# A routed-expert layer on one core: the query projection split into two passes, with gathers in the second

## The chip, the cores and the metric

The kernel runs on one core of a Trainium2 chip. The metric is device time in microseconds (us); lower is better. The core has the engines PE (matrix products), DVE and ACT (elementwise work), POOL (elementwise work, and the issue of gathers) and SP (which here issues most DMAs). Each engine works through its instructions in a fixed order.

## What is computed

One decoder layer on 512 tokens of width 2048 in float32: attention with two groups of heads, then PEER, a layer of 16384 experts of one neuron each. The edit lies in PEER. Per token, 8 heads each pick 16 experts by product keys:

```python
q = (xt @ w_query).reshape(T, PEER_HEADS, 2, PEER_HALF)        # 2048 -> 16 x 128
scores = jnp.einsum('thpc,hpnc->thpn', q, sub_keys)            # 128 keys for each half
vals, idx = lax.top_k(scores, PEER_TOPK)
cand = vals[..., 0, :, None] + vals[..., 1, None, :]
top_vals, top_c = lax.top_k(cand.reshape(T, PEER_HEADS, 256), PEER_TOPK)
experts = i1 * PEER_N_KEYS + i2                                # 128 experts a token
gates = jax.nn.softmax(top_vals, axis=-1)
...
hdn = jax.nn.gelu(jnp.einsum('ted,td->te', expert_down[ec], xc))
y = jnp.einsum('te,ted->td', gc * hdn, expert_up[ec])
```

## The kernel before, in words

The 512 tokens are four blocks of 128. Matrix products are made with three passes of a split operand: `load_split` loads a raw piece of 128x1024 weights, ACT writes its rounded part `hi` (L93), and DVE or POOL writes the remainder `lo` (L94); `mm3` then runs lo by hi, hi by lo and hi by hi (L99 to L101). One ring of buffers, the pool `wts` (three raw, two hi, two lo), serves all weights up to the expert-up weights.

PEER works in two ways at once. The first 320 tokens meet all 16384 experts as dense products: 128 down tiles of 128 experts (`down_tile`, PSUM tile `dn`, 48 matmuls of 320 columns), then up products (`up`) against the activations times a dense gate matrix. The last 192 tokens gather their own experts' rows: the last 64 tokens of block 2 (list "e", spread over 128 partitions, 64 steps for each table) and block 3 (list "g", 128 steps for each table). One `gather_step` issues an indirect DMA of 128 rows, 1 MiB, from POOL (L511), and one DVE instruction of 2048 columns uses them (L517 for down rows, L525 for up rows). There are 384 steps. Four row buffers rotate; a step is tied in order to a matmul that is passed to it.

The stages that matter, as they are written:

- Choosing. For each of 8 heads, `queries(hp)` projects all 512 tokens for one half-key (48 matmuls of 512 columns into `pq`), keeps the columns of blocks 0 and 1 in `kept` and hands those of blocks 2 and 3 on as `qt`. `choose` makes scores (L562), takes the top 16 on DVE (MAX8, MATCH_REPLACE8, FIND_INDEX8; L539 to L543), forms candidates (L577), takes their top 16 and looks their numbers up (L587 to L590; half of the L589 products are on POOL). Blocks 2 and 3 of head hh are chosen, then blocks 0 and 1 of head hh - 1. The lists for the gathers are whole after the last head of blocks 2 and 3 (L618 to L623).
- Gates. For 10 chunks of 32 tokens, DVE makes one-hot tiles (L680, L681), ACT scales them, PE multiplies them (`gm`) and ACT copies them to a staging tile that goes to DRAM. One gather step in each of the 40 rounds.
- 28 down tiles whose results are spilled to DRAM (both `lo` pieces on POOL), then 10 that are held (`lo` on POOL and DVE, one gather step each).
- The expert loop, 16 groups of 16 slots: each slot loads 512 KiB of up weights and makes 24 matmuls of 320 columns; in every second of the first 180 slots a down tile is made as well, in the other 76 slots a spilled one is loaded back. Gather steps are issued at 1.6 a slot, then 0.8. The last quarter of the last group closes the output rows.

The written order is not the order of the engines: the framework in which the kernel is written lays out each engine's instructions ahead of the run, and places a later instruction earlier where its inputs and buffers allow it.

Of the kernel before, what the change touches and what calls it, by code (L numbers as in the profile page):

```python
# [8 lines left out]
F32 = mybir.dt.float32  # L9
# [9 lines left out]
P = 128  # L19
S = 512  # L20
NB = S // P
D = 2048
NK = D // P
# [6 lines left out]
PH = 8  # L30
TK = 16
HK = PH * TK
NE1 = 128
NEXP = NE1 * NE1
GC = 32
# [4 lines left out]
GB = NB - 1  # L40
NE = 64
EB = GB - 1
RB = 2
E0 = P - NE
ER = P // NE
EH = 128 // ER
HOLD = 10
SPILL = 28
# [11 lines left out]
def peer_block(ctx, tc, x, x_t, w_qk, w_v, w_fg, w_o, w_pq, sub_keys, down_t, down, up_t, up,  # L60
# [17 lines left out]
    ahead = []  # L78

    def fetch(src, pool):  # L80
        raw = pool.tile([P, 1024], F32, tag="raw", name="raw", bufs=3)
        DMA.dma_start(raw, src)
        return raw

# [354 lines left out]
    def aux(name):  # L439
        return psum.tile([P, S], F32, tag="aux", name=name, bufs=4)  # L440
# [89 lines left out]
    with tc.tile_pool(name="route", bufs=1, side="right") as rp:  # L530
        iota = rp.tile([P, NCAND], F32, name="iota_c")
        G.iota(iota, pattern=[[1, NCAND]], base=0, channel_multiplier=0, allow_small_or_imprecise_dtypes=True)
        sk = rp.tile([P, 2 * PH, NE1], F32, name="sk")
        DMA.dma_start(sk, sub_keys)

        def top16(vals, idx, src, width, nm):

            rest = rp.tile([P, width], F32, tag=f"rest{width}", name=f"rest_{nm}", bufs=3)
            V.max(vals[:, 0:8], src)  # L539
            V.match_replace(rest, vals[:, 0:8], src, NEG)  # L540
            V.max(vals[:, 8:16], rest)
            V.max_index(idx[:, 0:8], vals[:, 0:8], src)
            V.max_index(idx[:, 8:16], vals[:, 8:16], rest)  # L543

        def gate_exp(hh, bs):

            t = top[:, bs, hh]
            tmx = rp.tile([P, RB, 1], F32, name="tmx", bufs=2)
            V.tensor_copy(tmx, t[:, :, 0:1])
            V.tensor_tensor(t, t, tmx.broadcast_to([P, RB, TK]), ALU.subtract)  # L550
            A.activation(t, t, AF.Exp)

        def choose(hh, b0, queries):

            bs = slice(b0, b0 + RB)
            vals, idxf = [], []
            for half in range(2):
                hp = 2 * hh + half
                qt = queries(hp)
                sc = aux(f"sc{hp}{b0}")  # L560
                for b in range(RB):
                    PE.matmul(sc[:, b * P:(b + 1) * P], qt[:, b * P:(b + 1) * P], sk[:, hp], start=True, stop=True)  # L562
                vv = rp.tile([P, RB, TK], F32, name="vv", bufs=4)
                ii = rp.tile([P, RB, TK], U32, name="ii", bufs=2)
                for b in range(RB):
                    top16(vv[:, b], ii[:, b], sc[:, b * P:(b + 1) * P], P, f"{hp}{b0}{b}")
                fi = rp.tile([P, RB, TK], F32, name="fi", bufs=4)
                V.tensor_scalar(fi, ii, 128.0 if half == 0 else 1.0, None, ALU.mult)
                vals.append(vv)
                idxf.append(fi)  # L570
            cand = rp.tile([P, RB, NCAND], F32, name="cand", bufs=2)
            cex = rp.tile([P, RB, NCAND], F32, name="cex", bufs=2)
            for dst, (a, b) in ((cand, vals), (cex, idxf)):
                o = 0
                for i, n, m in CAND:
                    dd = dst[:, :, o:o + n * m].rearrange("p b (n m) -> p b n m", n=n)
                    V.tensor_tensor(dd, a[:, :, i:i + n].unsqueeze(3).broadcast_to([P, RB, n, m]),  # L577
                                    b[:, :, 0:m].unsqueeze(2).broadcast_to([P, RB, n, m]), ALU.add)
                    o += n * m
            pos = rp.tile([P, RB, TK], U32, name="pos", bufs=2)  # L580
            for b in range(RB):
                top16(top[:, b0 + b, hh], pos[:, b], cand[:, b], NCAND, f"c{hh}{b0}{b}")
            posf = rp.tile([P, RB, TK], F32, name="posf", bufs=2)
            V.tensor_copy(posf, pos)
            for b in range(RB):
                oh = rp.tile([P, TK, NCAND], F32, name="oh", bufs=2)
                V.tensor_tensor(oh, iota.unsqueeze(1).broadcast_to([P, TK, NCAND]),  # L587
                                posf[:, b].unsqueeze(2).broadcast_to([P, TK, NCAND]), ALU.is_equal)
                (V if hh == PH - 1 or b % 2 else G).tensor_tensor(oh, oh, cex[:, b].unsqueeze(1).broadcast_to([P, TK, NCAND]), ALU.mult)  # L589
                V.tensor_reduce(ex[:, b0 + b, hh], oh, AX.X, ALU.add)  # L590
            if hh:
                gate_exp(hh - 1, bs)
            if hh == PH - 1:
                gate_exp(hh, bs)
                den = rp.tile([P, RB, PH], F32, name="den", bufs=2)
                V.tensor_reduce(den, top[:, bs], AX.X, ALU.add)
                V.reciprocal(den, den)
                V.tensor_tensor(top[:, bs], top[:, bs], den.unsqueeze(3).broadcast_to([P, RB, PH, TK]), ALU.mult)

        kept = rp.tile([P, 2 * PH, RB * P], F32, name="kept")  # L600

        def queries(hp):
            ps = aux(f"pq{hp}")
            for piece in range(2):
                hi, lo = load_split(w_pq[hp, :, piece * 1024:(piece + 1) * 1024], G if hp else V)
                for kk in range(8):
                    k = piece * 8 + kk
                    sl = slice(kk * P, (kk + 1) * P)
                    mm3(ps, (hi[:, sl], lo[:, sl]), (hn[0][:, :, k], hn[1][:, :, k]), k == 0, k == NK - 1)
            qt = rp.tile([P, RB * P], F32, name="qt", bufs=2)  # L610
            A.copy(qt, ps[:, RB * P:])
            A.copy(kept[:, hp], ps[:, :RB * P])
            return qt


        for hh in range(PH):
            choose(hh, NB - RB, queries)
            if hh == PH - 1:  # L618
                for dst, src in ((gidx_e, ex), (gate_e, top)):
                    for r in range(ER):  # L620
                        V.tensor_copy(dst[r * NE:(r + 1) * NE], src[E0:, EB].rearrange("p h k -> p (h k)")[:, r * EH:(r + 1) * EH])
                V.tensor_copy(gidx, ex[:, GB])
                V.tensor_copy(gate_g, top[:, GB].rearrange("p h k -> p (h k)"))  # L623
            if hh:
                choose(hh - 1, 0, lambda hp: kept[:, hp])
        choose(PH - 1, 0, lambda hp: kept[:, hp])
    if "ex" in dbg:
        DMA.dma_start(dbg["ex"], ex)
        DMA.dma_start(dbg["gate"], top)
# [69 lines left out]
    with tc.tile_pool(name="exp", bufs=1, side="right") as xp:  # L699
# [78 lines left out]
        due = 0.0  # L778
# [16 lines left out]
        for g in range(NE1 // NG):  # L795
# [8 lines left out]
            for c in range(NK):  # L804
                raw = xp.tile([P, NG, P], F32, tag="uraw", name="uraw", bufs=3)
                DMA.dma_start(raw, up_t[g, c])
                uh = xp.tile([P, NG, P], F32R, tag="uhi", name="uhi", bufs=2)
                ul = xp.tile([P, NG, P], F32R, tag="ulo", name="ulo", bufs=2)
                A.activation(uh, raw, AF.Copy)  # L809
                V.tensor_tensor(ul, raw, uh.bitcast(F32), ALU.subtract)  # L810
                ps = aux("up")
                for j in range(NG):
                    mm = mm3(ps[:, :ND], (uh[:, j], ul[:, j]), pp[j], j == 0, j == NG - 1)
                if g == 0:
                    V.tensor_copy(yacc[:, c], ps[:, :ND])
                else:
                    V.tensor_tensor(yacc[:, c], yacc[:, c], ps[:, :ND], ALU.add)
                e = HOLD + g * NG + c // 2
                if c % 2 and e < NE1:
                    if e < NE1 - SPILL:  # L820
                        down_tile(e, (V, V))
                    else:
                        hold[e] = hold_p.tile([P, ND], F32, tag="hold", name=f"hold{e}")
                        DMA.dma_start(hold[e], hid_d[e - (NE1 - SPILL)])
                if c % 2 and (g + 1) * NG + c // 2 < NE1:
                    gate_tile((g + 1) * NG + c // 2)
                due += 1.6 if e < NE1 - SPILL else 0.8
                while due >= 1:
                    gather_step(mm)
                    due -= 1  # L830
                if g == NE1 // NG - 1 and c == NK - 1:
                    assert gstep[0] >= len(steps)
                if g == NE1 // NG - 2 and c == 4:
                    fin_load()
                if g == NE1 // NG - 1 and c % 4 == 3:
                    fin_quarter(c // 4)
# [74 lines left out]
```

## Time and profile before

| | |
|---|---|
| median of 3 runs | 3319.63 us (3317.11 to 3323.86) |
| profiled execution | 3313.15 us, span 3311.4 us |
| busy share PE, DVE, ACT, POOL | 94%, 75%, 37%, 29% |
| mean granted TensorE clock | 0.976 of full speed |
| DMA | 846.5 MB, 256 GB/s over the span |

All stages below are parts of the span of the profiled execution, in us from its start. A busy share is an average over stages with different limits, so each stage is read by itself; a PE that is busy can still run at half its clock.

### The profile page before, as it was taken

The page shows a single profiled execution, that of the slowest core. Times are in us where ns is not written, and L with a number is a line of the kernel's source. Part 1 is how long each engine was busy: PE and PEld are TensorE (multiplying, and loading weights), DVE is VectorE, ACT ScalarE, POOL GpSimd, SP SyncE. Part 2 cuts the span into 40 slices and gives each one's busy share as a digit, 9 for nine tenths or more (in the row PEclk, how much of TensorE's full clock was granted, in tenths as well). Part 3 has the DMA queues.
Part 4 walks back from the last instruction along what each step waited for, and adds up shares of the span by engine and source line. Part 5 has one row for each costly group of instructions (what it writes and reads, how often), then busy time and mean ns, then how long its engine had stood idle before and what let it go on. Part 6 is the DMA issues. An engine that isn't in the chain of part 4 may idle for free.

```text
span 3311.4 us, 47208 instructions
## 1 busy us (share of the span) xinstructions
PE 3098.8 (94%) x18265; PEld 2828.8 (85%) x18265; DVE 2497.5 (75%) x3724; ACT 1214.8 (37%) x1863; POOL 967.6 (29%) x529
## 2 busy tenths in 40 slices
PE   6999999999998877889999999999999999998987
PEld 4887778878876667778999999999999999998877
DVE  5225665454357899992799998998999999988885
ACT  4224444343231117884333333332333333322233
POOL 2000000000024445766434433333433344432210
PEclk9999999999999889999999999999999999999999
DMA  4322222214432136887799999999999999999983
GB/s 178 98 94 75 69 69 73 70 62 137 130 128 71 64 116 239 323 331 266 278 391 388 394 397 365 396 402 359 378 404 392 397 396 404 374 377 366 349 307 117
DMA packets 215792, 846.50 MB, mean 256 GB/s; under 512 B 20944, under 2 KB 69456, under 8 KB 163216
## 3 DMA queue, kind: packets, MB, share of 16 engines
q1 hardware_dynamic: 159424, 439.37, 37.1%
q0 software_dynamic: 55296, 402.68, 30.5%
q8 instruction: 143, 2.34, 0.3%
q10 hardware_dynamic: 848, 1.44, 0.1%
q14 instruction: 81, 0.66, 0.1%
HBM read 806.31 MB, written 35.91 MB: 254 GB/s over the span
## 4 chain that ended last, share of the span: by engine, by line
PE 42%; DVE 11%; issue 5%; DMA 3%; POOL 2%; ACT 0%; SPq 0%; ACTq 0%; DVEq 0%; POOLq 0%
PE up L99 7%; PE up L100 7%; PE up L101 7%; PE dn L99 7%; PE dn L100 7%; PE dn L101 6%; DVE o L680 2%; DMA uraw<-in_up_t 2%; DVE o L681 2%; DVE rows L517 2%; DVE ulo L810 1%; DVE yg_g L525 1%; POOL rows L511 1%; POOL lo L94 1%; DVE hn L802 1%
## 5 line engine op out<-in xcount | busy, mean ns | idle before, releaser
L93 ACT ACTIVATE hi<-raw 128x1024 fp32r<-128x1024 f32 x416 | 439.8, 1058 | 733.1 <-PE dn L101 221.9
L99 PE MATMUL up<-hn,ulo 128*128 128x320 f32 x2048 | 646.6, 316 | 55.6 <-DVE ulo L810 55.1
L99 PE MATMUL dn<-hn,lo 128*128 128x320 f32 x2048 | 650.3, 318 | 44.3 <-POOL lo L94 41.8
L94 DVE TENSOR_TENSOR lo<-raw,hi 128x1024 fp32r<-128x1024 f32 x320 | 390.1, 1226 | 352.9 <-ACT hi L93 351.9
L100 PE MATMUL dn<-hn,hi 128*128 128x320 f32 x2048 | 647.2, 316 | 0.0
L101 PE MATMUL dn<-hn,hi 128*128 128x320 f32 x2048 | 645.6, 315 | 0.0
L100 PE MATMUL up<-hn,uhi 128*128 128x320 f32 x2048 | 640.3, 313 | 0.9 <-DVE hn L802 0.9
L101 PE MATMUL up<-hn,uhi 128*128 128x320 f32 x2048 | 639.6, 312 | 0.0
L809 ACT ACTIVATE uhi<-uraw 128x1024 fp32r<-128x1024 f32 x256 | 271.7, 1061 | 648.8 <-PE up L101 504.5
L99 PEld LDWEIGHTS up<-hn,ulo 128*128 128x128 f32 x2048 | 390.9, 191 | 70.4 <-DVE ulo L810 66.0
L99 PEld LDWEIGHTS dn<-hn,lo 128*128 128x128 f32 x2048 | 388.9, 190 | 54.1 <-POOL lo L94 50.5
L100 PEld LDWEIGHTS up<-hn,uhi 128*128 128x128 f32 x2048 | 391.2, 191 | 1.2 <-DVE hn L802 1.2
L101 PEld LDWEIGHTS up<-hn,uhi 128*128 128x128 f32 x2048 | 390.9, 191 | 0.0
L100 PEld LDWEIGHTS dn<-hn,hi 128*128 128x128 f32 x2048 | 389.2, 190 | 0.0
L101 PEld LDWEIGHTS dn<-hn,hi 128*128 128x128 f32 x2048 | 388.8, 190 | 0.0
L810 DVE TENSOR_TENSOR ulo<-uraw,uhi 128x1024 fp32r<-128x1024 f32 x256 | 309.3, 1224 | 49.4 <-PE dn L99 28.6
L511 POOL DMA_INDIRECT rows<-in_up,gidx x128 | 222.9, 1741 | 401.9 <-DVE yg_g L525 380.1
L511 POOL DMA_INDIRECT rows<-in_down,gidx x128 | 209.5, 1637 | 379.1 <-DVE rows L517 347.2
L94 POOL TENSOR_TENSOR lo<-raw,hi 128x1024 fp32r<-128x1024 f32 x96 | 246.3, 2571 | 209.2 <-ACT hi L93 209.0
L525 DVE SCALAR_TENSOR_TENSOR yg_g<-rows,coef_g,yg_g 128x2048 f32<-128x2048 f32 x127 | 298.0, 2347 | 0.0
L517 DVE SCALAR_TENSOR_TENSOR rows<-rows,hng_g 128x2048 f32<-128x2048 f32 x128 | 290.7, 2286 | 3.9 <-DMA rows<-in_down,gidx 2.3
L99 PE MATMUL mm<-xn,lo 128*128 128x512 f32 x512 | 204.5, 399 | 0.0
(259 smaller groups left out, 5003.3 us busy)
## 6 DMA issues: line engine op xcount, KB each, us to landing
raw<-in_down_t SPq DMA_DIRECT2D x256, 512.0 KB
uraw<-in_up_t SPq DMA_DIRECT2D x256, 512.0 KB
raw<-in_w_qk SPq DMA_DIRECT2D x64, 512.0 KB
g_d<-stg SPq DMA_DIRECT2D x10, 2048.0 KB
gt<-g_d SPq DMA_DIRECT2D x32, 640.0 KB
raw<-in_w_v SPq DMA_DIRECT2D x32, 512.0 KB
raw<-in_w_o SPq DMA_DIRECT2D x32, 512.0 KB
raw<-in_w_pq SPq DMA_DIRECT2D x32, 512.0 KB
```

The lines of the kernel that those rows point to most:

```text
L93: A.activation(hi, raw, AF.Copy)
L94: (lo_on or V).tensor_tensor(lo, raw, hi.bitcast(F32), ALU.subtract)
L99: PE.matmul(ps, a[1], b[0], start=first, stop=False)
L100: PE.matmul(ps, a[0], b[1], start=False, stop=False)
L101: return PE.matmul(ps, a[0], b[0], start=False, stop=last)
L511: ld = G.indirect_dma_start(out=rows, out_offset=None, in_=table, in_offset=bass.IndirectOffsetOnAxis(ap=ix[:, j:j + 1], axis=0))
L517: use = V.scalar_tensor_tensor(rows, rows, 1.0, hng[part], ALU.mult, ALU.mult, accum_out=dots[part][:, j:j + 1])
L525: use = V.scalar_tensor_tensor(yg[part], rows, coef[part][:, j:j + 1], yg[part], ALU.mult, ALU.add)
L680: V.tensor_tensor(o2, iob, col(i2t), ALU.is_equal)
L681: V.tensor_tensor(o1, iob, col(i1t), ALU.is_equal)
L809: A.activation(uh, raw, AF.Copy)
L810: V.tensor_tensor(ul, raw, uh.bitcast(F32), ALU.subtract)
```

## The change

The query projection is made twice, for half of the tokens each time. The first pass runs all eight heads for blocks 2 and 3, then the lists for the gathers are copied, then the second pass runs all eight heads for blocks 0 and 1, with two gather steps behind each head. The query matmuls have 256 columns in place of 512; the 32 pieces of query weights are loaded and split twice. They go into buffers in the choosing's own pool `rp` (two raw, two hi, two lo) and no longer through the ring `wts`; the tile `kept` is gone. In the expert loop the pace of the gathers is 1.52 and 0.7 a slot in place of 1.6 and 0.8.

```diff
     def fetch(src, pool):
-        raw = pool.tile([P, 1024], F32, tag="raw", name="raw", bufs=3)
+        raw = pool.tile([P, 1024], F32, tag="raw", name="raw", bufs=3 if pool is wts else 2)
...
-        kept = rp.tile([P, 2 * PH, RB * P], F32, name="kept")
-        def queries(hp):
-            ps = aux(f"pq{hp}")
-            for piece in range(2):
-                hi, lo = load_split(w_pq[hp, :, piece * 1024:(piece + 1) * 1024], G if hp else V)
...
-                    mm3(ps, (hi[:, sl], lo[:, sl]), (hn[0][:, :, k], hn[1][:, :, k]), k == 0, k == NK - 1)
-            A.copy(qt, ps[:, RB * P:])
-            A.copy(kept[:, hp], ps[:, :RB * P])
+        def queries(b0):
+            def of(hp):
+                ps = aux(f"pq{hp}{b0}")[:, :RB * P]
+                cg = slice(b0 * P // GC, (b0 + RB) * P // GC)
+                for piece in range(2):
+                    hi, lo = load_split(w_pq[hp, :, piece * 1024:(piece + 1) * 1024], G if hp else V, rp)
...
+                        mm = mm3(ps, (hi[:, sl], lo[:, sl]), (hn[0][:, cg, k], hn[1][:, cg, k]), k == 0, k == NK - 1)
+                A.copy(qt, ps)
+                last[0] = mm
...
         for hh in range(PH):
-            choose(hh, NB - RB, queries)
...
-            if hh:
-                choose(hh - 1, 0, lambda hp: kept[:, hp])
-        choose(PH - 1, 0, lambda hp: kept[:, hp])
+            choose(hh, NB - RB, queries(NB - RB))
...
+        for hh in range(PH):
+            choose(hh, 0, queries(0))
+            for _ in range(2):
+                gather_step(last[0])
...
-                due += 1.6 if e < NE1 - SPILL else 0.8
+                due += 1.52 if e < NE1 - SPILL else 0.7
```

## Rows read from the trace of the kernel before

**Rows 1.** The page's forty slices of the span, busy tenths.
```profile
PE   6999999999998877889999999999999999998987
...
DVE  5225665454357899992799998998999999988885
```

**Rows 2.** Stretches: length, busy us (instructions) by engine, granted clock, DMA share, GB/s.
```profile
966.90:1256.00 289.10, 233.80 (x1012) 188.67 (x1011) 242.02 (x1168) 54.82 (x89) 123.30 (x55) 0.90 0.25 84
1256.00:1504.00 248.00, 205.67 (x1365) 193.48 (x1366) 246.51 (x163) 205.28 (x446) 164.25 (x71) 0.94 0.83 311
1504.00:1578.00 74.00, 69.41 (x451) 66.66 (x450) 3.75 (x4) 26.37 (x32) 45.16 (x20) 1.00 0.74 249
1578.00:1651.00 73.00, 72.79 (x471) 69.65 (x470) 54.35 (x45) 26.34 (x38) 33.06 (x20) 1.00 0.78 275
1651.00:2947.00 1296.00, 1280.36 (x8588) 1273.90 (x8588) 1205.35 (x1157) 445.42 (x548) 507.53 (x287) 0.99 1.00 389
2947.00:3217.00 270.00, 237.25 (x1503) 227.60 (x1501) 231.34 (x224) 72.87 (x85) 63.48 (x46) 0.95 0.94 351
```

**Rows 3.** Timeline, first loads, scores and down tile: start, us, engine, line.
```profile
913.23 17.13 SPq L82 DMA_DIRECT2D raw<-in_w_pq  x4
...
960.90 0.34 SPq L534 DMA_DIRECT2D sk<-in_sub_keys  x1
...
965.91 0.97 PE L562 MATMUL sc<-sk,qt 128*128 128x128 f32 x4 [2.86 <-DMA sk<-in_sub_keys]
...
966.91 0.30 DVE L539 MAX8 vv<-sc 128x8 f32<-128x128 f32 x1 [10.60 <-PE sc L562]
...
1203.94 0.42 PE L99 MATMUL dn<-hn,lo 128*128 128x320 f32 x1 [1.76 <-POOL lo L94]
```

**Rows 4.** Groups by line, 966.9 to 1256, the splits: busy us, mean ns.
```profile
L94 POOL TENSOR_TENSOR lo<-raw,hi 128x1024 fp32r<-128x1024 f32 x36 | 87.4, 2430 | 80.6 <-ACT hi L93 80.6
...
L93 ACT ACTIVATE hi<-raw 128x1024 fp32r<-128x1024 f32 x37 | 39.3, 1062 | 129.5 <-issue 129.5
```

**Rows 5.** Two stretches of unbroken matmuls: pq alone, then the expert loop.
```profile
951.40:962.70 11.30, 11.26 (x48) 1.00 0.61 175
...
1700.00:1750.00 50.00, 50.00 (x341) 50.00 (x340) 46.22 (x43) 15.99 (x18) 14.42 (x12) 1.00 1.02 404
```

**Rows 6.** Timeline of DVE while experts are chosen.
```profile
1066.92 2.26 DVE L589 TENSOR_TENSOR oh<-oh,cex 128x800 f32<-128x800 f32 x1
...
1073.04 0.30 DVE L539 MAX8 vv<-sc 128x8 f32<-128x128 f32 x1 [0.80 <-PE sc L562]
...
1088.04 1.29 DVE L549 COPY tmx<-top 128x2 f32<-128x2 f32 x1
...
1107.06 0.30 DVE L539 MAX8 vv<-sc 128x8 f32<-128x128 f32 x1 [0.80 <-PE sc L562]
...
1216.06 1.88 DVE L589 TENSOR_TENSOR oh<-oh,cex 128x800 f32<-128x800 f32 x2
```

**Rows 7.** Timeline of DVE while gates are built.
```profile
1404.34 1.22 DVE L680 TENSOR_TENSOR o<-iota_e,i2t 128x1024 f32<-128x1024 f32 x1
...
1408.82 3.40 DVE L680 TENSOR_TENSOR o<-iota_e,i2t 128x1024 f32<-128x1024 f32 x1
```

**Rows 8.** Groups by line, 1256 to 1504: busy us, mean ns.
```profile
L517 DVE SCALAR_TENSOR_TENSOR rows<-rows,hng_e 128x2048 f32<-128x2048 f32 x40 | 99.8, 2496 | 0.0
...
L94 POOL TENSOR_TENSOR lo<-raw,hi 128x1024 fp32r<-128x1024 f32 x31 | 89.9, 2912 | 42.2 <-ACT hi L93 42.0
...
L680 DVE TENSOR_TENSOR o<-iota_e,i2t 128x1024 f32<-128x1024 f32 x40 | 75.7, 1894 | 1.4 <-PE gm L687 1.0 <-ACT i2t L667 0.4
...
L681 DVE TENSOR_TENSOR o<-iota_e,i1t 128x1024 f32<-128x1024 f32 x40 | 74.7, 1867 | 0.0
```

**Rows 9.** Stretches, matmuls of the down tiles alone: PE busy us (matmuls).
```profile
951.40:1256.00 304.60, 28.62 (x168) 0.90 0.27 91
1256.00:1504.00 248.00, 156.03 (x716) 0.94 0.83 311
```

More of the change, by code (lines that the diff above doesn't have):

```diff
@@ L598, in choose @@
                 V.tensor_tensor(top[:, bs], top[:, bs], den.unsqueeze(3).broadcast_to([P, RB, PH, TK]), ALU.mult)
-        kept = rp.tile([P, 2 * PH, RB * P], F32, name="kept")
-        def queries(hp):
-            ps = aux(f"pq{hp}")
-            for piece in range(2):
-                hi, lo = load_split(w_pq[hp, :, piece * 1024:(piece + 1) * 1024], G if hp else V)
-                for kk in range(8):
-                    k = piece * 8 + kk
-                    sl = slice(kk * P, (kk + 1) * P)
-                    mm3(ps, (hi[:, sl], lo[:, sl]), (hn[0][:, :, k], hn[1][:, :, k]), k == 0, k == NK - 1)
-            qt = rp.tile([P, RB * P], F32, name="qt", bufs=2)
-            A.copy(qt, ps[:, RB * P:])
-            A.copy(kept[:, hp], ps[:, :RB * P])
-            return qt
@@ L616, in peer_block @@
-        for hh in range(PH):
-            choose(hh, NB - RB, queries)
[L618 to L623, printed above, removed]
-            if hh:
-                choose(hh - 1, 0, lambda hp: kept[:, hp])
@@ L626, in peer_block @@
-        choose(PH - 1, 0, lambda hp: kept[:, hp])
+        def queries(b0):
[4 more added lines that the diff above has]
+                    hi, lo = load_split(w_pq[hp, :, piece * 1024:(piece + 1) * 1024], G if hp else V, rp)
+                    for kk in range(8):
+                        k = piece * 8 + kk
+                        sl = slice(kk * P, (kk + 1) * P)
+                        mm = mm3(ps, (hi[:, sl], lo[:, sl]), (hn[0][:, cg, k], hn[1][:, cg, k]), k == 0, k == NK - 1)
+                qt = rp.tile([P, RB * P], F32, name="qt", bufs=2)
+                A.copy(qt, ps)
+                last[0] = mm
+                return qt
+            return of
@@ new lines, in peer_block @@
+        last = [None]
+        for hh in range(PH):
+            choose(hh, NB - RB, queries(NB - RB))
+        for dst, src in ((gidx_e, ex), (gate_e, top)):
+            for r in range(ER):
+                V.tensor_copy(dst[r * NE:(r + 1) * NE], src[E0:, EB].rearrange("p h k -> p (h k)")[:, r * EH:(r + 1) * EH])
+        V.tensor_copy(gidx, ex[:, GB])
+        V.tensor_copy(gate_g, top[:, GB].rearrange("p h k -> p (h k)"))
+        for hh in range(PH):
+            choose(hh, 0, queries(0))
+            for _ in range(2):
+                gather_step(last[0])
```

## The prediction

> **What bounds the kernel now.** I read the page's forty slices first, then a table of busy time by stretch, then the rows inside the stretches that the edit touches. The slices [rows 1] show that from a third of the span on either PE or DVE stands at 9 tenths in nearly every slice; PE dips only where DVE is full. The stretch table [rows 2] says where one engine waits for the other:
>
> - 966.9 to 1256, choosing experts: DVE 242 of 289 us, PE 234 busy at a granted clock of 0.90 (its two levels, 1.2 and 2.4 GHz, averaged). DVE leads here.
> - 1256 to 1504, building gates with 40 gather steps: DVE 246.5 of 248 us. DVE is the bound; PE fills in expert-down tiles.
> - 1504 to 1578: DVE 3.75 us of 74, PE 69. Here PE finishes the 28 spilled down tiles alone. 1578 to 1651 are the ten held ones. These 147 us are what the first half hands on to the expert loop.
> - 1651 to 2947: PE 1280 of 1296 us with DMA at a share of 1.00. Both are full.
> - 2947 to 3217: PE 237 of 270, DMA 0.94, DVE 231. The gathers load DMA and DVE more than PE is loaded.
>
> So the second half can gain only from fewer gathers; the first half has about 100 us of idle PE before 1504 and 70 us of idle DVE behind it. The question is whether the edit lets the two overlap. A row shows what keeps them apart: the first down tile's matmul runs at 1203.94 [rows 3], directly behind the last query matmul, although nothing of the choosing is an input to it. Down tiles take their raw, hi and lo buffers from the same ring as the query weights, whose entries are written earlier in the program. The program text alone does not hold the order: the down tiles are written behind the choosing, which lasts to 1256, and behind the gates.
>
> **The change, part by part.**
>
> *Start.* The first query weights are issued at 913.23, into the ring [rows 3]. With the change they lie in the choosing's own pool; before, the first load into that pool is issued at 960.90 (sk), and PE is released by it at 965.91, 5.0 us for 1 MB. So I put the first weights at 967, behind sk on SP's queue. A split on ACT (1.06 us [rows 4]) and one on DVE, 48 matmuls (5.6 us, below), copy and scores follow, by estimate 9.5 us: the first DVE MAX8 comes at 976.5 in place of 966.91. **+10 us.** Behind the waiting load on SP stand the next query pieces and any down loads; PE waits for those, or has down tiles.
>
> *PE's query work.* 48 matmuls of 512 columns take 11.26 us, 0.2346 us each; 341 of 320 columns take 50 us, 0.1466 each [rows 5]. The slope is 0.458 ns a column, so 256 columns cost 0.117 us. Twice 768 at 0.117 is 180 us, once 768 at 0.2346 also 180. **0.** No row has a stream of 256 columns; the bounds are 0.117 and 0.1466 (no faster than 320), 45 us of PE, which has over 100 to spare here.
>
> *Choosing on DVE.* Two choices take 34.0 us (MAX8 at 1073.04 and again at 1107.06 [rows 6]), 17.0 each; 16 of them 272 us (289 by the whole stretch is the upper bound, since in it the first head ran alone).
>
> *The second split of the weights.* 32 pieces more: 30 on POOL at 2.43 us [rows 4], two on DVE. POOL was busy 123 of 289 us [rows 2], so its time is there. But they cost DVE: its L589 takes 0.94 us in a pair with POOL idle and 2.26 beside a POOL split; L549, a copy of two columns, takes 1.29 beside one [rows 6]. In that 34 us period four splits cost DVE about 4.2 us, 1.06 each. In the gates the same splits cost more: L680 is 1.22 alone and 3.40 beside one [rows 7], and 40 of each operation took 250 us where alone (2.28, 1.22 and 1.22) they need 189; 61 us over 31 splits is 2.0 each [rows 8]. Bounds 0 and 2.0; I take 1.06, the value from this stage. 30 x 1.06 + 2 x 1.22 = **+34 us.** The Trainium skill ("SBUF — State Buffer", section "Who interferes with whom") says that a VectorE instruction with two SBUF inputs and a GpSimd instruction that reads SBUF exclude each other for their whole length, whoever starts first. The 3.40 us agree with it; that rule speaks against this change, and its full price is rival B.
>
> *Sixteen gathers into the second pass.* DVE 2.28 + 0.08 us each: **+38 us** here. POOL has room to issue them; behind an issue that waits for a row buffer stand POOL's splits, and PE waits for those.
>
> *Removed: the kept copies*, on ACT, 55 us busy of 289: **0**, hidden; ACT's added hi splits (32 x 1.06) hide there too.
>
> Choosing would so end at 976.5 + 272 + 34 + 38 = 1321, without tiles.
>
> *Down tiles in the idle PE.* A tile is 48 matmuls, 7.04 us, and two splits on POOL. From 951 to about 1360 PE has 409 us, 200 of them for queries and (by estimate 20) scores: room for 29 tiles. In the gates, with 101 us of its own (205.67 less 716 at 0.1466), PE had room for 21 and took 716/48 = 15 [rows 9]. The same 70% gives 20; 3.5 of them ran there before. Of the 40 splits each costs DVE 1.06, 42 us: choosing ends at **1363** (+107).
>
> *Gates.* 8 spilled tiles are left in place of 15; half of the ten held ones follow into the freed PE time (none and all are the bounds). Splits on POOL 21 in place of 31: -20; five splits on DVE +6. 248 - 14 = 234: end at **1597**. Left are five held tiles, 36 us where 147 stood: the expert loop begins at **1633** in place of 1651. **-18 us.**
>
> *Expert loop.* The pace falls from 1.6 to 1.52 steps a slot for 180 slots (288 to 273.6 gathers of 1 MiB) and from 0.8 to 0.7 for the 76 behind. In the first part PE is at 99%; 8588 matmuls at 0.1466 are 1259 of 1296 us, so at most 37 us come back, and I take 5. In the second, 270 us hold 1503 matmuls, one tile and 60.6 slots, 4.34 us a slot against 3.52 for 24 matmuls; a tenth of a gather at 351 GB/s is 0.30 us: -18, and the gathers end 3 slots later, +1. Together **-22** (bounds 0 and -54). A later end of the gathers leaves 12.6 slots, over 40 us, for the closing of the last block.
>
> Sum: -18 - 22 = -40. The profiled execution took 3313.15 us (span 3311.4 and 1.75 around it), 6.5 below the median of 3319.63; so 3273, as a median **3280 us**.
>
> **The rivals.**
>
> *A: the down tiles stay behind the choosing* (slower). Behind the gates a spilled tile took 7.7 us (74 us for 9.6), and DVE saves 2.1 for each that stays. With n tiles brought forward (up to 13; the gates take 15) the loop begins at 1321 + 2.1n + 248 + 7.7(13 - n) + 73 = 1742 - 5.6n; with the loop's -22 it breaks even at n = 12. With none: +91 - 22, 3389 us. For it: only 3.5 tiles ran there before. Against it: these ran as soon as the ring was free, and the ring is now theirs from the last output weights on.
>
> *B: POOL's splits hold DVE at the price of the gates* (slower). At 2.0 us the 70 splits more cost 66 us more: +26, 3346 us. It decides from 1.6 us a split. For it: L680's 3.40. Against it: most of the choosing's instructions are MAX8 and FIND_INDEX8, and only some of its rows show a longer time. This is what the skill's rule gives if the splits always meet two-input instructions.
>
> *C: the splits fall beside such instructions and cost nothing*: 74 us less, 3206.
>
> *D: no change that can be measured.* All ten held tiles stay behind the gates (37 us more there, 16 less of splits in them: +21), and the loop's slots get hardly shorter: 3313 to 3326. A measurement of this kernel tells no change below 0.2%, 6.6 us.
>
> **How the numbers follow.** Forecast 0.45 (3240 to 3312), C 0.10, D 0.15, A 0.15, B 0.15. The range must hold 0.8: it leaves out most of C (0.08) and the far part of A (0.12), 3235 to 3350. Faster by over 0.2%: forecast, C and a little of D, 0.58; within it 0.12; slower: A, B, the rest of D, 0.30.
>
> **What would show it.** In the new profile: dn matmuls from some 955 on, about 20 tiles before the choosing ends near 1363; pq matmuls 0.117 us apart; the first MAX8 near 976; choices 19 us apart in the first pass; L680 nearer to 1.22 us; hardly any stretch with DVE below a tenth; the first up matmul near 1633; slots of about 4.0 us at the end. Wrong: fewer than 12 tiles before the choosing ends, DVE idle for scores because PE stands in order behind a tile's late split, or slots of the loop no shorter.

## The result and the profile after

The changed kernel takes 3338.72 us (median of 5 runs, 3336.3 to 3345.93) where the kernel before takes 3319.63: a ratio of 1.0065, 95% interval 1.0049 to 1.008. It is slower. The profiled execution took 3345.93 us, the longest of the five, span 3343.9 against 3311.4. So the stages below add up to 32.5 us, of which some 20 are what the medians show; the rest is spread between executions and isn't put down to any stage.

The page's forty slices after the change, to be held against [rows 1]:

```profile
PE   6999999999998777788999998999999999998897
DVE  5225665454348999999589888999999999988895
```

Then the stretches that answer to [rows 2]; columns as there.

```profile
986.20:1347.00 360.80, 275.20 (x1950) 262.08 (x1950) 338.81 (x1200) 110.92 (x144) 243.12 (x107) 0.93 0.51 171
1347.00:1590.00 243.00, 199.99 (x1327) 186.79 (x1328) 241.88 (x162) 202.68 (x438) 157.93 (x70) 0.94 0.86 314
1590.00:1628.00 38.00, 35.16 (x236) 34.09 (x234) 8.04 (x6) 16.23 (x26) 21.84 (x9) 1.00 0.92 320
1628.00:1697.00 69.00, 66.40 (x430) 63.52 (x430) 56.40 (x49) 27.64 (x39) 32.03 (x19) 1.00 0.89 309
1697.00:2991.00 1294.00, 1279.95 (x8625) 1273.58 (x8624) 1183.90 (x1129) 445.70 (x547) 481.17 (x274) 1.00 0.99 380
2991.00:3253.00 262.00, 230.43 (x1482) 223.33 (x1481) 215.41 (x220) 75.88 (x92) 55.92 (x41) 0.96 0.91 332
```

The choosing of experts now has DVE busy 339 of 361 us and POOL 243, where DVE had 242 of 289 and POOL 123. The dip of DVE behind the gates is still there, shorter: 38 us with 8 busy in place of 74 with 4. To compare exactly, both traces are cut at four events: DVE's first MAX8 on scores, its last reduction of the choosing, its last one-hot of the gates, and the first up matmul, with which the expert loop begins; each counts by its start.

| us | before | after | difference |
|---|---|---|---|
| first MAX8 | 966.91 | 986.18 | +19.3 |
| choosing | 285.7 | 357.6 | +71.9 |
| gates | 244.0 | 247.4 | +3.4 |
| behind the gates | 157.8 | 106.5 | -51.3 |
| expert loop to the end | 1657.0 | 1646.2 | -10.8 |

Between the two events of the choosing DVE was busy for 336.0 us in place of 238.8 and idle for 22 in place of 47: its own work grew by 97 us. DVE's way to the end of the gates grew by 94.6 us, and the stretch behind them, where PE finishes the down tiles, paid back half of that. The down tiles' matmuls alone, first ahead of 966.20, then in the choosing (from 20 us ahead of the first MAX8), in the gates and behind them (columns PE, weight loads, ACT, then clock, DMA share, GB/s):

```profile
900.00:966.20 66.20, 9.39 (x60) 8.95 (x61) 0.44 (x1) 0.95 0.39 122
966.20:1343.80 377.60, 72.00 (x415) 64.56 (x415) 3.49 (x8) 0.93 0.54 176
1343.80:1591.20 247.40, 153.09 (x711) 114.35 (x710) 6.78 (x15) 0.94 0.85 311
1591.20:1697.70 106.50, 100.26 (x644) 95.40 (x642) 5.74 (x13) 1.00 0.90 312
```

60 and 415 matmuls are 9.9 tiles ahead of the gates (3.2 in the kernel before, up to the same event); 13.4 are left behind them. The start, from the timeline of SP, ACT, PE and DVE:

```profile
916.04 18.35 SPq L82 DMA_DIRECT2D raw<-in_down_t  x4
...
965.52 0.46 SPq L534 DMA_DIRECT2D sk<-in_sub_keys  x1
966.03 0.90 SPq L82 DMA_DIRECT2D raw<-in_w_pq  x2
...
976.54 1.06 ACT L93 ACTIVATE hi<-raw 128x1024 fp32r<-128x1024 f32 x1 [3.00 <-issue]
979.45 1.06 ACT L93 ACTIVATE hi<-raw 128x1024 fp32r<-128x1024 f32 x1 [1.86 <-DMA raw<-in_w_pq]
...
979.76 0.28 PE L99 MATMUL pq<-hn,lo 128*128 128x256 f32 x1
...
980.48 0.28 PE L99 MATMUL pq<-hn,lo 128*128 128x256 f32 x1
...
986.18 0.30 DVE L539 MAX8 vv<-sc 128x8 f32<-128x128 f32 x1 [4.42 <-PE sc L562]
```

The ring's early slots went to down tiles (916.04, where query weights stood at 913.23 in [rows 3]); the two pieces of the first half-key are issued behind sk at 966.03, and split at 976.54 and 979.45. Six matmuls of 256 columns take 0.72 us, 0.12 each. Finally the groups by line in the choosing, DVE's and the splits on POOL:

```profile
L589 DVE TENSOR_TENSOR oh<-oh,cex 128x800 f32<-128x800 f32 x18 | 52.6, 2932 | 0.0
L587 DVE TENSOR_TENSOR oh<-iota_c,posf 128x800 f32<-128x800 f32 x32 | 38.7, 1249 | 0.0
L517 DVE SCALAR_TENSOR_TENSOR rows<-rows,hng_e 128x2048 f32<-128x2048 f32 x16 | 36.5, 2279 | 0.0
...
L542 DVE FIND_INDEX8 ii<-vv,sc 128x8 uint32<-128x128 f32 x64 | 18.3, 285 | 0.0
...
L550 DVE TENSOR_TENSOR top<-top,tmx 128x32 f32<-128x32 f32 x15 | 9.5, 635 | 0.0
...
L94 POOL TENSOR_TENSOR lo<-raw,hi 128x1024 fp32r<-128x1024 f32 x74 | 190.5, 2590 | 66.3 <-ACT hi L93 54.7 <-DMA raw<-in_w_pq 11.4
```

74 splits in place of 36 [rows 4]. The longer DVE instructions are the two-input ones, copies and casts (L549 to L589 without the searches, L577 as count times mean: 129.3 us before, 190.6 after; L589 2.93 us each against 2.11, L550 0.64 against 0.17). MAX8, MATCH_REPLACE8 and FIND_INDEX8 (L542 0.285, before 0.288) are what they were.

### The profile page after: what moved, and what is told of

The parts are those of the page before. It is cut to its first block, busy times and chain, and to the rows that moved or that the text cites. A ratio compares the mean times of both kernels' runs of the same rounds, so it can differ in the third digit from the quotient of the medians.

```text
span 3343.9 us, 48895 instructions
## 1 busy us (share of the span) xinstructions
PE 3103.7 (93%) x19033; PEld 2868.6 (86%) x19033; DVE 2564.1 (77%) x3726; ACT 1265.6 (38%) x1907; POOL 1035.2 (31%) x559
## 4 chain that ended last, share of the span: by engine, by line
PE 70%; DVE 14%; issue 5%; DMA 5%; POOL 4%; ACT 1%; SPq 0%; ACTq 0%; DVEq 0%; POOLq 0%
PE up L99 8%; PE up L100 8%; PE up L101 8%; PE dn L99 7%; PE dn L100 7%; PE dn L101 7%; PE mm L101 4%; PE mm L100 4%; PE mm L99 4%; POOL lo L94 3%; DVE o L683 2%; DVE rows L517 2%; PE po L100 2%; PE po L99 2%; PE po L101 2%
## 5 line engine op out<-in xcount | busy, mean ns | idle before, releaser
L93 ACT ACTIVATE hi<-raw 128x1024 fp32r<-128x1024 f32 x448 | 473.1, 1058 | 713.2 <-PE dn L101 228.7
L94 POOL TENSOR_TENSOR lo<-raw,hi 128x1024 fp32r<-128x1024 f32 x126 | 329.2, 2624 | 346.1 <-ACT hi L93 334.4
L511 POOL DMA_INDIRECT rows<-in_down,gidx x128 | 217.1, 1696 | 396.9 <-DVE rows L517 361.8
L517 DVE SCALAR_TENSOR_TENSOR rows<-rows,hng_g 128x2048 f32<-128x2048 f32 x128 | 290.2, 2284 | 12.0 <-DMA hng_g<-hn_d 6.8
```

What stands on the lines that cost most here:

```text
L93: A.activation(hi, raw, AF.Copy)
L94: (lo_on or V).tensor_tensor(lo, raw, hi.bitcast(F32), ALU.subtract)
L511: ld = G.indirect_dma_start(out=rows, out_offset=None, in_=table, in_offset=bass.IndirectOffsetOnAxis(ap=ix[:, j:j + 1], axis=0))
L517: use = V.scalar_tensor_tensor(rows, rows, 1.0, hng[part], ALU.mult, ALU.mult, accum_out=dots[part][:, j:j + 1])
```

## The experiments

Each starts from the changed kernel unless it says otherwise; ratios are to the kernel before, with 95% intervals.

**Tiles written between the choices.** The functions of the down tiles are moved ahead of the choosing.

```diff
             choose(hh, NB - RB, queries(NB - RB))
+            spill(1)
...
             choose(hh, 0, queries(0))
+            spill(2)
             for _ in range(2):
                 gather_step(last[0])
```

> The changed kernel, with the spilled down tiles written between the heads of the choosing (one behind each head of the first pass, two behind each head of the second, the last four behind the choosing). Theory order: the changed kernel loses because only 10 of its 28 spilled tiles run before the choosing ends, 107 us of tiles being left behind the gates. With 22 ahead the choosing lengthens by 12 x 2.1 = 25 us and the 107 us behind the gates fall to some 20: first up matmul near 1640 in place of 1698, time 3270 to 3290. Rival DVE: the first half is bound by DVE alone, each tile brought forward costs it as much as it saves: 3330 to 3345.

Measured 3350.12 us, 1.0095 [1.0062, 1.0129], above both ranges. That the program's order was all that stood in the way is refuted: the tiles did come forward, and it got slower. Choosing, gates and what is behind them, then the choosing's down matmuls (from 20 us ahead), by stretch:

```profile
986.00:1420.00 434.00, 376.28 (x2637) 363.58 (x2636) 359.74 (x1196) 161.58 (x199) 319.97 (x134) 0.95 0.55 180
1420.00:1654.00 234.00, 197.70 (x1301) 186.86 (x1300) 227.11 (x177) 194.32 (x425) 123.84 (x57) 0.93 0.85 318
1654.00:1708.00 54.00, 14.70 (x84) 13.51 (x83) 36.89 (x43) 17.38 (x35) 18.35 (x12) 0.71 0.92 352
...
966.30:1419.80 453.50, 178.24 (x1107) 166.73 (x1106) 10.06 (x23) 0.95 0.56 185
```

DVE's largest wait there, the same wait in the changed kernel, and the chain behind the gates of this run:

```profile
DVE vv L560 <- PE sc L583: 53.3, 20, 7.8
```
```profile
DVE vv L539 <- PE sc L562: 10.2, 3, 4.4
```
```profile
1659.29 4.65 DMA rows<-in_down,gidx_e
1663.95 10.34 DMA g_d<-stg
1674.35 15.69 DMA gt<-g_d
```

With 58 matmuls ahead of these rows 24.3 tiles ran ahead, 14.4 more than in the changed kernel, and the choosing took 433 us in place of 358: 5.3 us a tile. DVE's own work grew by 24 us (1.6 a tile); its wait for scores grew from 10 us to 53. PE runs in order, and a choice's queries now stand behind a tile; in the second pass PE was also near its own bound (busy for 220 of 247 us), and no run parts the two. And behind the gates 54 us remain, in which PE is busy for 15 at a granted clock of 0.71: the last gathered row, the store and the reload of the gates (26 us, with DMA at a share of 0.92) and the products behind them set the loop's begin.

**The query splits on DVE**, to free POOL: `load_split(..., V, rp)` for all pieces.

> The changed kernel, with the remainders of the query weights made on DVE in place of POOL in both passes. Theory order: DVE takes 60 x 1.22 = 73 us of work and is freed of 60 waits of some 1.3 us, so the choosing stays within 20 us of 361 plus what the tiles add; POOL is free for tiles, of which 18 come forward, and the stretch behind the gates falls from 107 to some 30 us: 3290 to 3310. Rival DVE: POOL's splits hold DVE by less than 1.22 us each, and the choosing lengthens by 50 us or more: 3350 to 3380.

3345.43 us, 1.0079 [1.0049, 1.0108], between the two ranges. With less for POOL to do, 920 down matmuls and 66 ahead of 967 ran ahead, 20.5 tiles, as many as the forecast wanted; choosing 413 us, that is 55 more, gates 237, 62 us behind them, loop at 1700.15. Twenty tiles ahead are to be had, and they don't pay.

**No gathers between**, the pace of before.

```diff
             choose(hh, 0, queries(0))
-            for _ in range(2):
-                gather_step(last[0])
```

> The changed kernel without the gather steps in the second pass, and with the pace of before (1.6 and 0.8 a slot). Theory order: the choosing shortens by 38 us, as 16 gathers were on DVE's path, the loop lengthens again by 11: 3305 to 3315, below the changed kernel but hardly below the kernel before, as the tiles are as few. Rival gathers: it is the gathers that make the changed kernel slow, and without them it is clearly faster than before, below 3300.

3323.97 us, 1.0023 [1.0008, 1.0039], above both ranges. Choosing 302.8 us, so the 16 gathers and what comes with them are 54.8 there, 3.4 each. L517 is 36.5 of it. But 2.4 tiles fewer ran ahead as well, by the first run's price some 13 of the 54.8, so the gathers' own share lies between 42 and 55. Lines L549 to L589 took 156.9 us here, 33.7 less than with gathers, at 69 POOL splits against 74. In the timeline of the changed kernel those beside a gather's issue alone are not longer (L549 0.14 us, L568 0.19); the long ones run beside splits. With the gathers between, the splits met more of them; why is not settled.

**Query weights through the ring again**: `rp` is left out of the call.

> The changed kernel with the query weights in the old ring in place of buffers of their own. Theory order: no tile can come forward (10 fewer than now, 5.6 us each at the loop's start, less some 20 us at the start of the choosing, where the first weights are early again): 3360 to 3385. Rival: the buffers change nothing but the start, 3315 to 3325.

3360.63 us, 1.012 [1.0088, 1.0152]. The first MAX8 is back at 966.42, and the tiles ahead fall to 4, with 150 us behind the gates and the loop at 1716.47. That lies in the theory's range. Buffers of their own put the first MAX8 20 us later and brought 5.9 tiles forward.

**No second split.** In the second pass all but the first half-key's pieces take `hi` for `lo`.

```diff
+        if skip:
+            A.activation(hi, raw, AF.Copy)
+            return hi, hi
```

> The changed kernel, without the remainder of the query weights in the second pass (the rounded part stands in for it, so the queries of blocks 0 and 1 lack two of their three passes' precision; all matmuls are still made). Theory port: POOL's splits hold DVE's two-input instructions. The choosing falls from 358 to 305 to 320 us, and of DVE's groups only L549, L550, L568, L577, L584, L587 and L589 get shorter; time 3295 to 3310. Rival lateness: the choosing is long because queries come late behind POOL, DVE's busy time stays at 338 us and its idle time falls.

3304.13 us, 0.9965 [0.9949, 0.998]. Choosing 327.3 us, with one tile more ahead: 30 splits are worth 30.3 us there, less than the theory's 38 to 53, and 35 us of the whole.

**A memset in their place**, on POOL, `G.memset(lo.bitcast(F32), 0.0)`, so that POOL stays occupied but reads nothing; `lo` is zero then.

> As the run without the second split, but POOL writes a memset of 128x1024 where it made the remainder (the remainder of the query weights in the second pass is zero). Theory port: a memset reads nothing from SBUF and does not hold DVE; the choosing is within 10 us of the run without the second split. Rival: whatever POOL does on that memory holds DVE, in proportion to POOL's time; the choosing stays over 335 us.

3307.86 us, 0.9971 [0.9958, 0.9983]. POOL's groups in the choosing:

```profile
L97 POOL TENSOR_TENSOR lo<-raw,hi 128x1024 fp32r<-128x1024 f32 x45 | 113.0, 2526 | 40.7 <-ACT hi L93 40.6
...
L95 POOL MEMSET lo<- 128x1024 f32 x30 | 28.5, 958 | 34.2 <-PE pq L102 19.1 <-DVE ii L546 8.1 <-PE pq L104 5.2
```

Choosing 327.0 us, as without them: 30 more instructions on POOL, with their waits, cost the stage nothing. In proportion to its time (0.96 us against 2.5) a memset would have cost what 0.4 splits do, 11.6 us for 30. So it is for the most part the split's reading that costs; a POOL instruction of 2.5 us that only writes was not run. Single DVE instructions do wait for a memset (lines are three higher here, L571 is L568 of the changed kernel):

```profile
1191.32 0.97 POOL L95 MEMSET lo<- 128x1024 f32 x1
1191.36 0.97 DVE L571 TENSOR_SCALAR fi<-ii 128x32 f32<-128x32 uint32 x1
```

This instruction of one input takes 0.17 us alone and here ends with the memset. Four such cases beside a memset alone, of this line and of the copy L552, add up to some 2.5 us; two-input instructions in front of them were not lengthened (L580, 0.16 us), those behind them waited in DVE's order.

**One projection**, from the kernel before: `kept` and the ring stay; the lists are copied between the passes and two gathers stand behind each head of the second.

> The order of the changed kernel (blocks 2 and 3 for all heads, then blocks 0 and 1 with two gathers behind each head, pace 1.52 and 0.7), but queries projected once with 512 columns into the old ring, and kept for the second pass, as before. Theory path (what sets the start of the loop is DVE's way through choosing and gates and some 50 us behind it): the first pass is PE's at 11.6 us a half-key, 186 us, the second DVE's with 16 gathers, 180; choosing ends near 1340 as in the changed kernel, 10 tiles go into the second pass, first up matmul 1640 to 1660, time 3285 to 3305. Rival: the order alone costs what the changed kernel costs, 3335 to 3350.

3332.1 us, 1.0042 [1.0025, 1.0059], between the two ranges. The two passes here, then in the changed kernel (columns as in [rows 2]):

```profile
966.80:1172.80 206.00, 197.64 (x883) 156.32 (x882) 124.16 (x583) 45.85 (x73) 93.60 (x40) 0.99 0.27 88
1172.80:1363.80 191.00, 134.50 (x727) 128.90 (x728) 189.57 (x610) 54.83 (x64) 112.20 (x55) 0.80 0.55 195
```
```profile
986.20:1146.20 160.00, 130.67 (x977) 123.74 (x978) 143.17 (x583) 52.88 (x70) 110.06 (x45) 0.98 0.45 144
1146.20:1343.80 197.60, 143.26 (x968) 137.34 (x968) 192.81 (x613) 56.83 (x71) 133.05 (x62) 0.89 0.57 196
```

Nothing is split twice, yet the choosing took 397 us: all queries fall into the first pass, and PE bounds it, busy for 198 of 206 us. The second pass, without queries or query splits, held 14 tiles in 191 us, where the changed kernel needed 198 with 5.3. In all 16 tiles ran ahead and the loop began at 1683.8, 14 us ahead of the changed kernel. So the second projection bought an even load in the first pass, and no time for the whole: the kernel without it is, if anything, the faster one.

**The old pace**, 1.6 and 0.8 a slot.

> The changed kernel with the pace of before, 1.6 and 0.8 gather steps a slot. If the loop's 11 us come from the 16 gathers that it no longer holds, the time stays within 5 us of the changed kernel (3334 to 3344); if they come from the pace, it is 3345 to 3352.

3340.75 us, 1.0064 [1.0047, 1.0081]: the pace is worth nothing. The loop took 1638.2 us. In the kernels with 16 gathers in the choosing and all 38 tiles made ahead of the loop it took 1638 to 1646; with all gathers behind the choosing (the third run, the last two and the kernel before) it took 1651.6 to 1660.2, so the fewer gathers give the loop its 11 us.

Three runs looked for a version that computes everything and beats both. **`lo` kept in DRAM**: the first pass stores it, the second loads it, with no second split.

```diff
+                    if b0:
+                        hi, lo = load_split(src, G if hp else V, rp)
+                        DMA.dma_start(lo_d[hp, piece], lo.bitcast(F32))
+                    else:
...
+                        DMA.dma_start(lo.bitcast(F32), lo_d[hp, piece])
+                        A.activation(hi, raw, AF.Copy)
```

> The changed kernel, but the remainders of the query weights are written to DRAM in the first pass and loaded from there in the second; POOL makes each only once. Theory port: the 30 splits of the second pass are gone as in the run without them, the choosing is 320 to 335 us in place of 358, time 3300 to 3315. Rival DMA: 32 MB more in 360 us at a share of 0.54 delay the weights and the gathers, and the choosing stays over 350 us.

3358.14 us, 1.0116 [1.0096, 1.0137]. In the choosing's waits, DVE waits for PE, and PE for the reload:

```profile
DVE vv L539 <- PE sc L562: 61.9, 12, 9.2
...
PE pq L99 <- DMA lo<-lo_d: 35.6, 14, 5.0
```

DVE's busy time fell to 298 us, but the choosing took 386, as the rival had it. The loop began at 1662.7, 47 us behind the gates, with 5.5 of the 38 tiles still to be made, and took 1681 us.

**The same with the first half-key's weights through the ring** in the first pass, `rp if hp else None`:

> As the run with the remainders in DRAM, and the weights of the first half-key go through the old ring, so that they are there when the hidden state is. Theory path: the first MAX8 comes at 967 to 972 in place of 985, and all behind it as much earlier, since DVE's way sets the start of the loop: 3285 to 3302. Rival: the 15 us are lost again behind the gates, where PE has as many tiles as before: 3300 to 3315.

3341.56 us, 1.0069 [1.0047, 1.0091], above both ranges; first MAX8 at 969.75, choosing 384. The loop began at 1643.3, 11 us ahead of the kernel before, with 6.5 tiles still to be made, and took 1697. An early first up matmul is not by itself time won.

**That without the gathers between**:

> As the run before it, without the gathers in the second pass and with the pace of before. Theory path: 16 gathers cost DVE's way about 50 us and give the loop 10; what stands behind the gates then is PE's tiles (128 us with 6 tiles ahead), so that half of it is seen: 3270 to 3290, clearly faster than both kernels. Rival: with DVE's way shorter PE alone sets the start of the loop, near 1640, and the gathers in the loop cost what they cost before: 3295 to 3310.

3320.19 us, 0.9998 [0.9981, 1.0015], above both ranges: no different from the kernel before.

**The changed kernel with the first half-key's first pass through the ring, no gathers between**, `rp if hp or not b0 else None`:

> The changed kernel without the gathers in the second pass, with the pace of before and with the first half-key's weights in the old ring; remainders made twice. Theory path: the first MAX8 at 967 to 972; 3308 to 3318, some 10 us below the run without gathers. If the start counts for nothing: 3320 to 3328.

3322.52 us, 1.001 [0.9994, 1.0026]. First MAX8 at 968.79, choosing 315.3, 133.9 us behind the gates: as the kernel before. Against the third run the first MAX8 came 13 us earlier and the choosing took 13 us longer, so the start counted for nothing here. No version that computes everything beat the kernel before.

## Why the prediction was wrong

The forecast was 3280 us; the measured 3338.72 lies on the other side of no change. The loop's begin was forecast 21 us early (1633 against 1654.38) and came 43 late. By the forecast's own marks: the choosing ended at 1343.8 for 1363 (-19), the gates took 247 for 234 (+13), and 106.5 us stood behind them for 36 (+70). The last is the failure.

**The step that failed: down tiles in the idle PE, and the 36 us left behind the gates.** Twenty tiles were expected in the choosing; 9.9 came. Rival A's line, 1742 - 5.6n, gives 1687 for them and 1720 for the 4 of the shared ring; measured 1697.7 and 1716.5. So A's mechanism decided, in the middle of its line: most tiles stayed behind. (That the line comes so near is in part luck: the start was 10 us later than it has it, and the choosing itself 7 us shorter.) Written ahead, 24 tiles came, and with POOL freed of the query splits 20, so both the written order and POOL's work held them back. But the fault lies deeper than the count. The forecast priced a tile in the choosing at 2.1 us of DVE. DVE's work was priced well (1.6), and DVE's waiting for PE was left out: with tiles in front of the queries it is 5.3 us a tile in all (first run). In the changed kernel itself this wait was small (10 us, 35 before), as only few tiles came. And the forecast let the stretch behind the gates shrink with the tiles, though 54 us of it are another chain's, the gates' way through DRAM (43 and 47 us stood there in the two runs with `lo` in DRAM and their gathers, so the floor may lie lower). With 54, 20 tiles ahead at the forecast's price, and the gates at the 234 us that it forecast and the first run had, would have put the loop at 1363 + 234 + 54 = 1651, 3 us ahead of before in place of 21. PE's tiles covered that way before, but the timeline of before has it: SP stores the last gates and loads the first back 11.7 us later, well behind the last one-hot (1496.62).

```profile
1505.32 0.33 SPq L692 DMA_DIRECT2D g_d<-stg  x1
1517.05 0.38 SPq L787 DMA_DIRECT2D gt<-g_d  x1
```

Of the forecast's signs of being wrong, fewer than 12 tiles and slots no shorter were seen (at the end 4.26 us a slot, reckoned as in the forecast: 4.34 before, about 4.0 forecast); DVE idle for scores was not.

**The start** was +19.3, not +10. The estimate had the first weights in SBUF at 967, behind sk. sk itself was issued 4.6 us later than before (965.52 against 960.90), and the weights behind it could be split only 10.5 and 13.4 us after their issue, with DMA at a share of 0.72 from 956 to 986. From the first split to MAX8 it was 9.6 us, as estimated. With the first weights through the ring, as the fourth and the twelfth run have them, MAX8 came at 966 and 969; what that is worth at the end of the choosing was nothing in the twelfth run.

**PE's query work at no cost**: right, 0.12 us for 256 columns against 0.117.

**The second split, 1.06 us each**: right as an average, 30.3 us for 30. Rival B's 2.0 was not seen in the choosing. The Trainium skill ("SBUF — State Buffer", section "Who interferes with whom") has the exclusion for two-input VectorE instructions against GpSimd instructions that read SBUF: L550 at 0.64 us against 0.17 agrees, as do the two-input instructions of the sixth run, which no memset lengthened by itself (L580, 0.16 us). That rule alone does not give the longer instructions of one input (L549, L568), beside splits and beside memsets; and FIND_INDEX8, whose rows name two inputs, stayed at 0.28. A split of 2.5 us cost 1.0 on average: most DVE instructions of the choosing, MAX8 among them, take no longer beside one.

**Sixteen gathers, +38**: too small; removing them gave back 54.8 us of the choosing, 42 of them at the least by the gathers themselves (the estimate at the third run). In exchange the loop gained 11 us, not 22: the pace, to which 18 us were ascribed, is worth nothing (eighth run).

**The kept copies at nothing, ACT's added splits hidden**: nothing in the runs speaks against it; ACT is busy 111 of 361 us.

**The gates**: 247 us, as before, since the same 15 tiles ran in them (711 matmuls against 716). Their one-hot operations stayed at 1.97 us (1.89 before), where the forecast wanted them nearer 1.22: with so few tiles taken forward, the splits of the others still met them.

**The rivals.** C is refuted by the fifth run. B's 2.0 was not reached, but against the kernel before the changed one shows 1.6 us for each of its 38 splits more (61.3 us on L549 to L589), the price from which B decides; so B has a part in the result, with the gathers, and how large it is stays open. D's time (3313 to 3326) was not reached; its picture of tiles left behind the gates was right and too mild.

## What to carry to other kernels

When one engine bounds a stage and another is idle in it, work moved to the idle engine is priced by what it does to the bounding one: here through the splits that hold it (1 us each) and, more, by making its inputs wait for an engine that is no longer idle. Before counting a stretch as time to be won, look for the chain under it that another engine's work has covered; a run that moves that work away shows its floor. And work that is made twice to balance two engines must be priced on the third that prepares it.

## What the runs showed of the hardware

A POOL instruction of 0.96 us that only writes SBUF (memset, 30 of them) left DVE's stage at 327.0 us against 327.3 without, though it held single instructions of one input to its own end (0.97 us in place of 0.17); one of 2.5 us that reads two tiles costs DVE 1.0 us in this mix. MAX8 and FIND_INDEX8 (0.28 us) were not lengthened by either. The mean price depends on what it meets: 33 more splits lengthened L549 to L589 by 27.6 us without gathers (0.8 each), 38 more by 61.3 with them (1.6 each). Streams of 256 columns of this type take 0.12 us a matmul at a granted clock of 1.00, near the line through 320 and 512 columns [rows 5], which gives 0.117.
